# One hybrid decoder layer: VectorE's work on a step's operands is issued behind that of the step before, in the down projection

## The chip, the cores and the metric

One core of a Trainium2 chip runs the whole kernel. TensorE multiplies, with products in PSUM (8 banks of 128x512 float32); VectorE, ScalarE and GpSimd work on elements; the queues of SP and ScalarE issue transfers (DMAs) between HBM and SBUF. Each engine takes its instructions in the order in which the program has them, and waits at one until its inputs are there. The metric is the device time of one execution in microseconds (us); of several runs the median counts.

## What is computed

A layer with three mixers side by side, and a gated MLP behind them:

```python
h = rms_norm(x, norm1_g) * (1 + sc1) + sh1
x = x + g1 * hybrid_mixer(h, ...)            # GLA, retention, stick-breaking
h = rms_norm(x, norm2_g) * (1 + sc2) + sh2
x = x + g2 * swiglu(h, wg, wu, wd)           # (silu(h wg) * (h wu)) wd
return rms_norm(x, final_g)
```

1024 tokens, width 1024, MLP width 2816, all in float32. The change concerns the last product, `(...) wd`, a matrix of 1024x2816 by one of 2816x1024.

## The kernel before

**The down projection.** The product of gate and up projection, called G here, is 1024 tokens by 2816; w_down is 2816 by 1024. Both are cut into halves, G by tokens and by alternate blocks of 128 of the inner dimension, w_down by columns, and the product of the 2x2 blocks is made with seven block products instead of eight (Strassen's scheme in Winograd's form), whose left operands are the blocks a11, a12, a22 and the sums s1 to s4, and whose right operands are blocks of w_down and sums of them. The stage before has written the left ones to HBM (`d_g`).

A *step* (p, j) is one of 4 passes and one of 11 pairs of blocks j; pass 0 makes one of the seven products, passes 1 to 3 two each. `flow` (L1257) lists the steps, (0,0) to (3,10). For each step a generator `prep_1`, `prep_67`, `prep_53` or `prep_24` (L1180 to 1213) prepares operands in two halves: up to its `yield` it issues loads on SP, of `d_g` blocks into tiles `whi` and `wlo` in turn (three of each) and of w_down into a tile `hb` (`b_raw`, four of them; pass 0 loads into `kb[j]`, tiles that in the rows are called `hh` and `hl`). Behind the `yield` VectorE makes two *combining* instructions, as here in pass 2:

```python
tt(DVE, rb[:, 1], rb[:, 0], kb[j], ALU.subtract)      # hb <- hb, hh (or hl)
tt(DVE, kb[j], kb[j], grow[:, :NH], ALU.mult)         # hh <- hh, grow
return [(opnd(ra[:, 0]), opnd(rb[:, 1])), (opnd(ra[:, 1]), opnd(rb[:, 0]))]
```

and then `opnd` (L1147) splits each of the four sources into a rounded part (a cast on ScalarE, L929) and the rest (a *subtract* on VectorE, in `tt`, L58), because a product is made from three matmuls of such parts (`mm3`, L67). The results lie in 18 operand slots used in turn: 12 tiles `to` and 6 pairs made of old `hh` and `hl`. In pass 3 one of the four operands, a12, is ready in HBM and is loaded straight into its slot (`opnd_of`, L1156). A combining instruction needs the load of its `hb`; a cast needs a free slot, that is, the matmuls over 18 operands before.

**Matmuls and adds.** A step makes, for each of its products and each of 4 blocks of 128 tokens, three 128x512 matmuls: 12 in pass 0, 24 in the others. The 4 or 8 PSUM banks of a pass (tiles `m`, `dn`, `tr`) gather all 11 steps. At the end of a pass they are added to `ct` in SBUF (VectorE, `ct<-ct,m` and the like; pass 0 copies them with ScalarE), and a bank is free for the next pass when this is done. Between the steps, residual additions and squares of finished output columns are made (`residual`, `second_columns`: `ct<-ct,grow`, `ct<-ct,raw`, `ct<-ct,st`), with the residual loaded into tiles `raw`. The last three steps of pass 3 are held back and made bank by bank, each followed by its final norm and store (the tail).

**What sets the order.** The program is traced step by step: loads are asked for six steps ahead, operands three steps ahead (four late in pass 3), through `finish` (L1276), which runs a generator's second half. A scheduler then puts each engine's instructions into an order by a simulated timeline of its own: an instruction whose inputs come early there may move ahead of others, also of those of earlier steps.

Of the kernel before, what the change touches and what calls it, by code (L numbers as in the profile page):

```python
# [1 line left out]

# [37 lines left out]
def tile_hybrid(ctx, tc, x, c, ada_w, ada_b, norm1_g, norm2_g, w_in, gla_wa2, gla_ba,  # L40
# [3 lines left out]
    PE, ACT, DVE, POOL = nc.tensor, nc.scalar, nc.vector, nc.gpsimd  # L44
# [10 lines left out]


    def tt(eng, o, a, b, op):
        eng.tensor_tensor(out=o, in0=a, in1=b, op=op)  # L58

    def sub_lo(lo, src, hi):  # L60
        tt(DVE, lo, src, hi.bitcast(F32), ALU.subtract)
# [33 lines left out]
    def rstd_of(dst, ss, n, w):  # L95
        t = const.tile([P, 8], F32, name="rs_t", bufs=2)
        POOL.tensor_scalar(t[:, :w], ss, 1.0 / n, EPS, op0=ALU.mult, op1=ALU.add)
        tt(POOL, dst, t[:, :w], mhalf[:, :w], ALU.pow)
# [20 lines left out]
    def w_load(src, shape, fold=None):  # L119
        nn = shape[1] * shape[2]  # L120
        raw = wp.tile([P, W_SLOT], F32, name="raw", bufs=2)[:, :nn].rearrange("p (a b) -> p a b", a=shape[1])
        if isinstance(src, list):
            n = shape[1] // len(src)
            for i, sr in enumerate(src):
                nc.sync.dma_start(raw[:, i * n:(i + 1) * n], sr)
        else:
            nc.sync.dma_start(raw, src)
        if fold is not None:
            tt(DVE, raw, raw, fold, ALU.mult)
        hi = wp.tile([P, W_SLOT], F32R, name="whi")[:, :nn].rearrange("p (a b) -> p a b", a=shape[1])  # L130
        lo = wp.tile([P, W_SLOT], F32R, name="wlo")[:, :nn].rearrange("p (a b) -> p a b", a=shape[1])
        split(hi, lo, raw)
        return hi, lo
# [785 lines left out]
    def halves(x):  # L919
        return x.rearrange("p (n c) -> p n c", n=2)  # L920
# [147 lines left out]
    for j in range(4):  # L1068
# [5 lines left out]
        for lst, r in ((t2, r22), (t3, r12), (t4, r21)):  # L1074
            op = halves(tp.tile([P, D], F32R, name="to"))
# [197 lines left out]

    loaded = {}

    def finish(gen):  # L1276
        try:
            next(gen)
        except StopIteration as e:
            return e.value  # L1280

    for n, (p_, j) in enumerate(flow):

        for q, jq in flow[n:n + 3 + (p_ == 3 and j > 4)]:
            if (q, jq) not in ready:
                if (q, jq) not in loaded:
                    loaded[q, jq] = passes[q](jq)
                    next(loaded[q, jq])
                ready[q, jq] = finish(loaded[q, jq])
# [94 lines left out]
```

## Time and profile before

| | us |
|---|---|
| median of 3 runs | 1334.87 (1334.02 to 1335.86) |
| the profiled execution | 1338.11 |
| its span, first to last instruction | 1336.3 |
| TensorE busy in the span | 1277.9 (96%) |
| VectorE, ScalarE, GpSimd busy | 883.8, 634.1, 521.9 |
| granted TensorE clock, mean | 0.984 of full |

The down projection takes the end of the span, from about 1109.5 us: pass 0 to 1139.5, pass 1 to 1199.8, pass 2 from 1205.0 to 1266.5, then pass 3 with its tail from 1312. In the views PE is TensorE, DVE VectorE, ACT ScalarE, POOL GpSimd, and SPq the queue of SP. A row of a timeline gives start and duration, and in brackets how long the engine had stood idle before it and what it waited for. A matmul row's duration covers its way through the array, so that what counts is the distance from start to start. Tile names stand without their numbers.

### The profile page before, as it was taken

The numbers are of one execution on the slowest core, as the hardware profiler recorded it, in microseconds if no ns is written. First come the engines' busy times: TensorE is split into PE (matmuls) and PEld (weight loads), VectorE is DVE, ScalarE is ACT, GpSimd is POOL, SyncE is SP. The second block draws the span as 40 slices with busy tenths as digits, with TensorE's granted clock in tenths as the row PEclk, the third lists the DMA queues.
The fourth block names the chain that finished last, engine by engine and source line by source line (L and its number), as shares of the span: only waits on it lengthen the run. The fifth ranks groups of instructions, "written<-read, shape, count | busy, mean of one in ns | idle before, by whom it ended". The sixth has DMA issues, their size and how long they took to land. (4 is left out here: it accounts for less than half of the span.)

```text
span 1336.3 us, 20162 instructions
## 1 busy us (share of the span) xinstructions
PE 1277.9 (96%) x7165; PEld 1095.7 (82%) x7165; DVE 883.8 (66%) x1381; ACT 634.1 (47%) x1254; POOL 521.9 (39%) x594
## 2 busy tenths in 40 slices
PE   6999989998999989988999999999999999999997
PEld 3779988898899988987978888888887888877776
DVE  2424566778867768896678665665565659959695
ACT  3647557766647635453564332332333325443343
POOL 1017425346524354672114555556545432000044
PEclk8999998999999999998999999999999999999999
DMA  9647445444423275122324334343343358834453
GB/s 325 208 140 219 137 111 175 126 109 142 132 81 95 70 232 174 54 82 95 106 103 135 110 111 134 103 137 131 103 133 110 106 190 300 282 118 155 150 186 148
DMA packets 144334, 192.33 MB, mean 144 GB/s; under 512 B 19837, under 2 KB 94918, under 8 KB 144234
## 3 DMA queue, kind: packets, MB, share of 16 engines
q1 hardware_dynamic: 113808, 150.65, 36.7%
q10 hardware_dynamic: 30426, 40.40, 8.5%
q8 instruction: 56, 0.92, 0.3%
q14 instruction: 44, 0.36, 0.1%
HBM read 141.13 MB, written 49.87 MB: 143 GB/s over the span
## 5 line engine op out<-in xcount | busy, mean ns | idle before, releaser
L68 PE MATMUL dn<-whi,hh 128*128 128x256 f32 (+1 forms) x768 | 225.2, 293 | 4.3 <-DVE s_u L431 2.3
L69 PE MATMUL dn<-wlo,hh 128*128 128x256 f32 (+1 forms) x768 | 224.6, 293 | 0.0
L70 PE MATMUL dn<-whi,hl 128*128 128x256 f32 (+1 forms) x768 | 222.3, 290 | 0.0
L68 PEld LDWEIGHTS dn<-whi,hh 128*128 128x128 f32 x768 | 149.7, 195 | 6.3 <-DVE hh L58 2.8
L69 PEld LDWEIGHTS dn<-wlo,hh 128*128 128x128 f32 x768 | 149.8, 195 | 1.6 <-issue 0.2
L70 PEld LDWEIGHTS dn<-whi,hl 128*128 128x128 f32 x768 | 149.4, 195 | 1.2 <-issue 0.2
L58 POOL TENSOR_TENSOR s_a<-s_a,s_u 128x128 f32<-128x128 f32 (+3 forms) x96 | 95.6, 998 | 95.1 <-DVE s_u L434 89.9
L434 DVE TENSOR_TENSOR_SCAN s_u<-z,s_u,zero 128x128 f32<-128x128 f32 (+3 forms) x96 | 96.3, 1008 | 35.8 <-ACT z L427 24.8
L58 POOL TENSOR_TENSOR st<-raw 128x512 f32<-128x512 f32 x40 | 57.9, 1449 | 112.3 <-DMA raw<-in_ffn_wg_dram 86.5
L58 POOL TENSOR_TENSOR x<-x,x 128x512 f32<-128x512 f32 x51 | 70.7, 1388 | 44.8 <-DVE x L58 37.5
L1238 POOL TENSOR_SCALAR ss<-ss 128x1 f32<-128x1 f32 x8 | 22.5, 2814 | 167.5 <-ACT raw L1234 166.9
L64 ACT CAST s_th<-tr 128x512 fp32r<-128x512 f32 (+2 forms) x112 | 48.6, 434 | 54.7 <-PE tr L451 29.3
L58 DVE TENSOR_TENSOR s_tl<-tr,s_th 128x512 fp32r<-128x512 f32 (+2 forms) x112 | 54.6, 487 | 28.1 <-ACT s_th L64 27.8
L929 ACT CAST wlo<-raw 128x512 fp32r<-128x512 f32 x34 | 20.9, 616 | 109.0 <-POOL x L58 82.3
L58 POOL TENSOR_TENSOR grow<-grow,a_raw 128x1024 f32<-128x1024 f32 x24 | 58.4, 2433 | 35.3 <-ACT a_raw L305 21.8
L58 DVE TENSOR_TENSOR wlo<-raw,wlo 128x512 fp32r<-128x512 f32 x34 | 24.5, 720 | 68.1 <-ACT wlo L929 68.1
L58 DVE TENSOR_TENSOR wlo<-st,wlo 128x512 fp32r<-128x512 f32 x40 | 41.2, 1032 | 37.1 <-ACT wlo L929 37.0
L426 ACT ACTIVATE s_a<-z 128x128 f32<-128x128 f32 (+3 forms) x96 | 47.1, 491 | 24.1 <-PE z L424 15.7
L68 PE MATMUL dn<-hh,whi 128*128 128x512 f32 x140 | 56.0, 400 | 1.4 <-ACT st L293 1.4
L70 PE MATMUL dn<-hh,wlo 128*128 128x512 f32 x144 | 56.4, 392 | 0.0
L69 PE MATMUL dn<-hl,whi 128*128 128x512 f32 x140 | 55.3, 395 | 0.0
L58 DVE TENSOR_TENSOR x<-x,m 128x512 f32<-128x512 f32 x68 | 45.6, 679 | 13.8 <-PE m L70 13.8
(395 smaller groups left out, 3830.9 us busy)
## 6 DMA issues: line engine op xcount, KB each, us to landing
a_raw<-in_ada_w_dram SPq DMA_DIRECT2D x24, 512.0 KB, 4.1
raw<-in_ffn_wg_dram SPq DMA_DIRECT2D x22, 512.0 KB, 3.8
raw<-in_ffn_wu_dram SPq DMA_DIRECT2D x22, 512.0 KB, 4.1
d_g_s<-x ACTq DMA_DIRECT2D x44, 256.0 KB, 2.2
hb<-in_ffn_wd_dram SPq DMA_DIRECT2D x44, 256.0 KB, 4.0
raw<-in_w_in_dram SPq DMA_DIRECT2D x20, 512.0 KB, 4.3
aw<-in_ada_w_dram SPq DMA_DIRECT2D x32, 256.0 KB, 6.0
d_g_a<-x ACTq DMA_DIRECT2D x22, 256.0 KB, 3.4
```

Source lines behind the costliest of these rows:

```text
L58: eng.tensor_tensor(out=o, in0=a, in1=b, op=op)
L64: ACT.copy(hi, src)
L68: PE.matmul(o, sh, mh, start=start, stop=False)
L69: PE.matmul(o, sh, ml, start=False, stop=False)
L70: PE.matmul(o, sl, mh, start=False, stop=stop)
L426: ACT.activation(At[:, c0:c0 + w], z[:, :w], AF.Sigmoid, scale=0.125)
L434: DVE.tensor_tensor_scan(ur, z[:, 0:w][:, ::-1], zero.broadcast_to([P, w]), u[:, w:w + 1], op0=ALU.mult, op1=ALU.add)
L929: ACT.copy(op[0], src)
L1238: POOL.tensor_scalar(ss2[t][:, 1:2], ss2[t][:, 1:2], 1.0 / D, EPS, op0=ALU.mult, op1=ALU.add)
```

## The change

`tt` now keeps the last instruction that it made on VectorE. When a step's preparation is over, `finish` notes that instruction, the last subtract of the step; everything that the next step's second half traces on VectorE is put behind the instruction noted last, by an order edge within the engine (`issue_after`). Such an edge carries no wait: it fixes which stands first in VectorE's queue. Loads, casts and the adds of PSUM banks have no such edge; the scheduler orders them anew around it.

```diff
     def tt(eng, o, a, b, op):
-        eng.tensor_tensor(out=o, in0=a, in1=b, op=op)
+        made_tt[eng is DVE] = eng.tensor_tensor(out=o, in0=a, in1=b, op=op)
+
+    made_tt = {}
...
     loaded = {}
 
+    done = []
+
     def finish(gen):
-        try:
-            next(gen)
-        except StopIteration as e:
-            return e.value
+        with (tc.issue_after(done[-1].ins) if done else nullcontext()):
+            try:
+                next(gen)
+            except StopIteration as e:
+                done.append(made_tt[True])
+                return e.value
```

Three places of VectorE's order follow. In the names, the `kb` tiles of pairs j = 0 to 5 are `hh_0_11562`, `hl_0_11572`, `hh_0_11582`, `hl_0_11592`, `hh_0_11596` and `hl_0_11600`, that of j = 10 is `hh_0_11718`.

VectorE at the turn from pass 1 to pass 2, before, from the last subtracts of step (2,1) on:

```order
L58 TENSOR_TENSOR to<-whi,to 128x512
L58 TENSOR_TENSOR to<-hb,to 128x512
L58 TENSOR_TENSOR to<-wlo,to 128x512
L58 TENSOR_TENSOR to<-hb,to 128x512
L58 TENSOR_TENSOR hb<-hb,hl_0_11600 128x512
L58 TENSOR_TENSOR hl_0_11600<-hl_0_11600,grow 128x512
L58 TENSOR_TENSOR to<-wlo,to 128x512
L58 TENSOR_TENSOR to<-hb,to 128x512
L58 TENSOR_TENSOR ct<-ct,m 128x512
```

The same place now, from the same two subtracts on:

```order
L58 TENSOR_TENSOR to<-whi,to 128x512
L58 TENSOR_TENSOR to<-hb,to 128x512
L58 TENSOR_TENSOR hb<-hb,hh_0_11582 128x512
L58 TENSOR_TENSOR hh_0_11582<-hh_0_11582,grow 128x512
L58 TENSOR_TENSOR to<-wlo,to 128x512
L58 TENSOR_TENSOR to<-hb,to 128x512
L58 TENSOR_TENSOR to<-wlo,to 128x512
L58 TENSOR_TENSOR to<-hb,to 128x512
L58 TENSOR_TENSOR hb<-hb,hl_0_11592 128x512
L58 TENSOR_TENSOR hl_0_11592<-hl_0_11592,grow 128x512
L58 TENSOR_TENSOR ct<-ct,m 128x512
```

The combining instructions of (2,5), and of (2,4) and (2,3) before them, no longer stand ahead of the first add; those of (2,2) and (2,3) come directly ahead of their own step's subtracts.

VectorE at the turn from pass 2 to pass 3, before: the combining instructions of (3,4), then of (3,5), with subtracts of (3,1) and (3,2) between and behind them.

```order
L58 TENSOR_TENSOR hb<-hb,grow 128x512
L58 TENSOR_TENSOR hb<-hb,hh_0_11596 128x512
L58 TENSOR_TENSOR to<-wlo,to 128x512
L58 TENSOR_TENSOR to<-hb,to 128x512 x2
L58 TENSOR_TENSOR hb<-hb,grow 128x512
L58 TENSOR_TENSOR hb<-hb,hl_0_11600 128x512
L58 TENSOR_TENSOR hl_1_12930<-whi,hh_1_12929 128x512
L58 TENSOR_TENSOR hl_1_12934<-hb,hh_1_12933 128x512
L58 TENSOR_TENSOR ct<-ct,m 128x512 x2
```

The same place now: step (3,2) whole, the two combining instructions of (3,3), and the adds.

```order
L58 TENSOR_TENSOR hb<-hb,grow 128x512
L58 TENSOR_TENSOR hb<-hb,hh_0_11582 128x512
L58 TENSOR_TENSOR to<-hb,to 128x512
L58 TENSOR_TENSOR hl_1_12930<-whi,hh_1_12929 128x512
L58 TENSOR_TENSOR hl_1_12934<-hb,hh_1_12933 128x512
L58 TENSOR_TENSOR hb<-hb,grow 128x512
L58 TENSOR_TENSOR hb<-hb,hl_0_11592 128x512
L58 TENSOR_TENSOR ct<-ct,m 128x512 x2
```

The combining instructions of (3,4) and (3,5) have moved behind the adds.

VectorE at the end of pass 3, before: the last rows ahead of the tail's first add.

```order
L58 TENSOR_TENSOR hb<-hb,hh_0_11718 128x512
L58 TENSOR_TENSOR to<-hb,to 128x512
L58 TENSOR_TENSOR ct<-ct,raw 128x512
L58 TENSOR_TENSOR ct<-ct,st 128x512
L58 TENSOR_TENSOR to<-wlo,to 128x512
L58 TENSOR_TENSOR to<-hb,to 128x512
L58 TENSOR_TENSOR ct<-ct,raw 128x512
L58 TENSOR_TENSOR to<-hb,to 128x512
L58 TENSOR_TENSOR ct<-ct,st 128x512 x2
L58 TENSOR_TENSOR ct<-ct,raw 128x512
L58 TENSOR_TENSOR to<-whi,to 128x512
L58 TENSOR_TENSOR to<-hb,to 128x512
```

The same place now: the whole of steps (3,9) and (3,10).

```order
L58 TENSOR_TENSOR hb<-hb,grow 128x512
L58 TENSOR_TENSOR hb<-hb,hl_0_11694 128x512
L58 TENSOR_TENSOR to<-hb,to 128x512
L58 TENSOR_TENSOR to<-wlo,to 128x512
L58 TENSOR_TENSOR to<-hb,to 128x512
L58 TENSOR_TENSOR hb<-hb,grow 128x512
L58 TENSOR_TENSOR hb<-hb,hh_0_11718 128x512
L58 TENSOR_TENSOR to<-hb,to 128x512
L58 TENSOR_TENSOR to<-whi,to 128x512
L58 TENSOR_TENSOR to<-hb,to 128x512
```

The residual work stands ahead of these steps now, and the combining instructions of (3,10) directly ahead of its three subtracts.

## Rows read from the trace of the kernel before

**Rows 1.** The page's first part: busy time, share, instructions of each engine.

```profile
PE 1277.9 (96%) x7165; PEld 1095.7 (82%) x7165; DVE 883.8 (66%) x1381; ACT 634.1 (47%) x1254; POOL 521.9 (39%) x594
```

**Rows 2.** By stretch: busy (count) of PE, PEld, DVE, ACT, POOL; clock; DMA; GB/s.

```profile
1139.50:1199.80 60.30, 60.17 (x265) 49.27 (x263) 46.48 (x76) 28.47 (x51) 0.00 (x0) 1.00 0.59 195
1266.50:1312.20 45.70, 44.35 (x193) 35.92 (x193) 41.28 (x69) 17.40 (x37) 22.51 (x8) 1.00 0.53 171
```

**Rows 3.** Waits of TensorE from 1099 us on: total, times, longest.

```profile
PE m L68 <- DVE ct L58: 5.0, 1, 5.0
PE m L68 <- DMA hh<-d_g_a12h: 1.1, 1, 1.1
```

**Rows 4.** Timeline of TensorE at the turn from pass 1 to 2: start, duration.

```profile
1194.85 0.39 PE L70 MATMUL m<-to 128*128 128x512 f32 x1
...
1199.61 0.39 PE L70 MATMUL m<-to 128*128 128x512 f32 x1
1205.01 0.77 PE L68 MATMUL m<-hh,hh 128*128 128x512 f32 x1 [5.01 <-DVE ct L58]
...
1208.32 0.39 PE L70 MATMUL m<-to 128*128 128x512 f32 x1
```

**Rows 5.** By stretch, as rows 2, just behind that wait.

```profile
1205.00:1208.40 3.40, 3.39 (x9) 2.72 (x10) 2.87 (x6) 0.00 (x0) 0.00 (x0) 0.56 0.61 210
```

**Rows 6.** Timeline of VectorE up to the turn from pass 1 to 2.

```profile
1175.39 0.69 DVE L58 TENSOR_TENSOR hb<-hb,hl 128x512 f32<-128x512 f32 x1 [2.03 <-DMA hb<-in_ffn_wd_dram]
...
1194.60 0.69 DVE L58 TENSOR_TENSOR hb<-hb,hh 128x512 f32<-128x512 f32 x1 [2.34 <-DMA hb<-in_ffn_wd_dram]
...
1196.54 0.68 DVE L58 TENSOR_TENSOR to<-hb,to 128x512 fp32r<-128x512 f32 x1
...
1201.64 0.69 DVE L58 TENSOR_TENSOR hb<-hb,hl 128x512 f32<-128x512 f32 x1 [3.21 <-DMA hb<-in_ffn_wd_dram]
...
1204.18 0.68 DVE L58 TENSOR_TENSOR ct<-ct,m 128x512 f32<-128x512 f32 x1
```

**Rows 7.** Timeline of SP's queue there: issue of the load for (2,5).

```profile
1197.54 0.38 SPq L1140 DMA_DIRECT2D hb<-in_ffn_wd_dram  x1
```

**Rows 8.** The tile `hb` from 1100 us on: waits for its loads, and landing times.

```profile
  DMA hb<-in_ffn_wd_dram: 29.9, 17
...
DMA to landing us min/median/max: 2.9/4.0/6.5
```

**Rows 9.** Timeline of ScalarE there: first cast of each half of (2,3).

```profile
1194.64 0.62 ACT L929 CAST to<-whi 128x512 fp32r<-128x512 f32 x1 [1.58 <-issue]
...
1197.36 0.62 ACT L929 CAST to<-whi 128x512 fp32r<-128x512 f32 x1 [1.58 <-issue]
```

**Rows 10.** Timeline of TensorE at the turn from pass 2 to 3.

```profile
1266.32 0.39 PE L70 MATMUL m<-to 128*128 128x512 f32 x1
...
1270.15 0.47 PE L68 MATMUL m<-hh,hh 128*128 128x512 f32 x1 [1.07 <-DMA hh<-d_g_a12h]
...
1271.39 0.39 PE L68 MATMUL m<-to 128*128 128x512 f32 x1
```

**Rows 11.** Timeline of VectorE there: the wait for (3,5), the last subtract of (3,2).

```profile
1262.88 0.69 DVE L58 TENSOR_TENSOR hb<-hb,grow 128x512 f32<-128x512 f32 x1 [2.26 <-DMA hb<-in_ffn_wd_dram]
...
1264.82 0.68 DVE L58 TENSOR_TENSOR hl<-hb,hh 128x512 fp32r<-128x512 f32 x1
```

**Rows 12.** Timeline of SP's queue there.

```profile
1265.53 0.33 SPq L1140 DMA_DIRECT2D hb<-in_ffn_wd_dram  x1
...
1266.43 0.38 SPq L1165 DMA_DIRECT2D hl<-d_g_a12l  x1
```

**Rows 13.** Timeline of TensorE at the turn from pass 0 to 1.

```profile
1142.64 0.39 PE L70 MATMUL m<-to 128*128 128x512 f32 x1
1143.16 0.50 PE L68 MATMUL tr<-to 128*128 128x512 f32 x1
```

**Rows 14.** By stretch, as rows 2: pass 3 until VectorE's operands are done.

```profile
1269.00:1309.50 40.50, 39.24 (x172) 32.07 (x172) 40.09 (x67) 16.78 (x36) 22.12 (x6) 1.00 0.55 176
```

More of the change, by code (lines that the diff above doesn't have):

```diff
@@ L1 @@
-from contextlib import ExitStack
+from contextlib import ExitStack, nullcontext
 import concourse.bass as bass
```

## The prediction

> **What bounds the kernel now.** The page's first part says that TensorE is the bound: busy for 1277.9 of 1336.3 us, VectorE for 883.8 [rows 1]. The change touches only the down projection, so the table by stretch comes next. There TensorE starts one matmul after another: 265 in the 60.3 us of pass 1, 0.2275 us from start to start; VectorE is busy for 46.5 of these 60.3 us, and for 41.3 of the 45.7 us of pass 3 before its last three steps [rows 2]. So only a hole in TensorE's row is worth anything in this stage. From 1099 us to the end TensorE has one long wait, 5.0 us for VectorE's `ct`, and short ones for loads of `a12`, the longest 1.1 us [rows 3].
>
> The long one stands at the turn from pass 1 to pass 2. The last matmul of pass 1 starts at 1199.61, the next one at 1205.01 [rows 4]; from then to 1208.4 the granted clock is 0.56, about 1.2 instead of 2.4 GHz, after the engine had stood still [rows 5]. What is waited for is a PSUM bank: `ct<-ct,m` adds the product of pass 1 into SBUF and frees the bank. Its matmuls were over at 1195.24 (the third starts at 1194.85 and takes 0.39) [rows 4], but the add ran at 1204.18 [rows 6], 8.9 us late. VectorE's own row says why: before it in the queue stand the two combining instructions of step (2,5), `hb<-hb,hl` and `hl<-hl,grow`, and the first sat 3.21 us until its load of w_down landed [rows 6]. That load was issued at 1197.54 [rows 7], right after VectorE's last subtract of step (2,1) (1196.54, 0.68 us) [rows 6], which gave its `hb` buffer back: there are four, so step j+4 loads into that of step j. The instruction is queued where its load cannot be there yet. Five such waits in a row, 2.0 to 3.2 us each and some 13 us together, lead up to the turn [rows 6]; in the whole down projection they are 17, 29.9 us [rows 8].
>
> **The change part by part.** No instruction is added or removed on any engine. VectorE's work on the operands of a step now stands behind the last subtract of the step before it, as the order listings show; loads keep their places on SP but for residual tiles and a few `hb`.
>
> (a) *From pass 1 to pass 2.* Ahead of the first `ct<-ct,m` the last combining instructions are now those of (2,3), no longer of (2,5). The casts that the subtracts follow go by TensorE's release of operand slots: the pairs at 1194.64 and 1197.36 are the two halves of (2,3), 2.72 us apart, which is 12 matmuls [rows 9]; the last pair of (2,2) is one beat earlier, at about 1191.9. With 0.60 us from one VectorE instruction to the next (67 in 40.1 us [rows 14]), (2,2) is through at about 1194, and (2,3)'s two combining instructions at about 1195.2. The load for (2,3) takes the buffer of (1,10), three steps of 5.46 us before; loads land after 4.0 us in the median [rows 8], so it is there. The add runs at about 1195.3, as its matmuls end, and the bank is free 4 us before TensorE asks. What is won: from the start at 1199.61 to that at 1208.32 lie nine starts and 8.71 us [rows 4]; at 0.2275 they take 2.05. **6.66 us**, 1.6 of it the slow clock.
>
> (b) *From pass 2 to pass 3.* From 1266.32 to 1271.39 TensorE has 13 starts in 5.07 us, at 0.2275 2.96: 2.11 us are lost, most where step (3,3) wants its `a12` at 1270.15 [rows 10]. That load stands on SP behind the `hb` load for step (3,6), which waits for VectorE's last subtract of (3,2): 1264.82 [rows 11], then `hb` at 1265.53 and the second half of `a12` at 1266.43 [rows 12]. VectorE was late because it had sat 2.26 us for the load of (3,5) [rows 11]. Nothing of (3,3) to (3,5) stands ahead of these subtracts now. Their casts are due three half steps before the pass ends, 8.2 us, so that the subtracts are through some 6.3 us before the end, not 1.7; `a12` comes 4.6 us earlier against the turn, and was short by 1.1. **2.11 us**; its bounds are 0 and 2.11, and I take the upper one, since the margin of 3.5 us is wide.
>
> (c) *From pass 0 to pass 1.* ScalarE copies two `tr` banks here, and now has one cast between the two copies. TensorE lost 0.29 us (0.52 from start to start) [rows 13]. The first bank comes free sooner, the second a cast (0.62 us [rows 9]) later: between -0.4 and +1 us, taken as 0, as the two work against each other.
>
> (d) *Where the order costs.* VectorE can no longer spend a wait for a cast on a later step's combining. In pass 1 it has room [rows 2], and operands are ready some four steps ahead (18 slots, four a step). Pass 3 is tight: in the listing of before, 70 instructions stand from the first add at the turn to the last ahead of the tail, and VectorE runs without rest from 1269 to 1309.5 [rows 14], where TensorE begins the last three steps at about 1312.3. Now 74 stand there, 44.4 us at 0.60; but they begin about 4.7 us before the turn, not 1.1. They end 39.7 us after it, and TensorE wants the last one 45 us after it: 5 us of cover. Cost: nothing.
>
> **Sum.** 6.66 + 2.11 = 8.77 us. The profiled execution took 1338.11 us, 1.81 beyond its span; it would take 1329.3. The runs' median is 1334.87, 3.24 lower. Of that, what is not the 1.81 may be shorter holes without the profiler; I take half of those 1.43 off the gain: 8.05 us, **1326.8**.
>
> **The rivals.**
> *Both turns mended*: 1326.8, between 1325.7 (the full gain, and the -0.4 of (c)) and 1329.3 (all of the 3.24 off the gain). Chance 0.60.
>
> *Only the first.* `a12` still lands after it is wanted, since SP keeps it behind the `hb` load, whose loads take up to 6.5 us [rows 8]. Against it: VectorE's late subtract held it, and that moves. 2.11 less: 1328.9. Chance 0.10.
>
> *The first in part.* A wait for a cast takes the place of that for a load: two subtracts of (2,3) stand between the first and the second add. If they came only with the second pair of casts (1197.36), the adds of all eight banks would end some 3 us after the turn, and half of the hole would stay: 1330 to 1332. Chance 0.08.
>
> *The holes are the profiler's.* VectorE's waits build up because a step takes it 7.04 us (1194.60 to 1201.64) [rows 6] where TensorE takes 5.46. The shortest load of `hb` took 2.9 us [rows 8]; if all did without the profiler, each of the five waits were 1.1 us shorter, the add 3.4 us late and not 8.9, which the 4.6 us between its matmuls' end and the end of the pass would swallow. Then the runs have no long hole to lose, and 2.1 us are won at most: 1332.8 to 1335.5. For it: loads spread from 2.9 to 6.5 us. Against it: the median of 4.0, and only 3.24 us lie between profile and runs. Chance 0.15. The Trainium skill (DMA: Bandwidth & Descriptors, Latency and other measured facts) says that a DMA's fixed cost shrinks as the load on HBM falls, with 0.2 us for an access on average and 2 us at high load. By that rule a run without the profiler's writes would lose up to 1.8 us of each load, an estimate from that page, and so the whole hole; no run here shows a load without the profiler.
>
> *Slower.* VectorE becomes the bound in pass 3. Before, it kept the waits for loads off the end by working ahead. If each of the six steps (3,5) to (3,10) still sat 2.3 to 3.2 us for its loads, 14 to 19 us would come to its 44.4, 9 to 14 beyond the cover, and TensorE would stand as long before its last steps and restart slowly (1.6): less 8.05, 1337.5 to 1342.5, say 1339.5. It decides from 5 us of such waits on. Against it: a load is issued when VectorE is done four steps earlier, 16 us ahead of its use in step order. Chance 0.07.
>
> That the order isn't what the change says is ruled out by the listings.
>
> **How the numbers follow.** A measurement of this kernel can tell about 0.2% (2.7 us) from nothing. Faster by more: 0.60 + 0.10 + 0.08 and a fifth of the profiler's case, 0.81. Same 0.12, slower 0.07. The range starts at 1324.5, 1325.7 less some 1 us, by which single runs lie under their median, and reaches over the third case to 1333.0; it leaves out the slower case and most of the profiler's.
>
> **What would show it.** Right: TensorE has no wait for `ct` after 1099 us; no stretch between the passes under clock 1; the first `ct<-ct,m` runs within 1 us of the end of its matmuls; VectorE's waits for `hb` loads fall from 29.9 us to a few, and waits for ScalarE's casts take their place; `a12` of (3,3) lands before it is wanted. Wrong: a wait of TensorE for an operand (`to`, `hl`) in pass 3, or VectorE's last subtract within 1 us of TensorE's last three steps; or a span shorter by 9 us while the runs are not.

## The result

The changed kernel takes 1328.17 us in the median of five runs (1323.22 to 1329.29), the kernel before, run beside it, 1335.12 (1334.02 to 1338.21). That is 6.95 us less by the medians. The ratio of the two kernels' runs is 0.994, with a 95% interval of 0.9921 to 0.9958: some 8 us less (5.6 to 10.5), where 8.05 had been forecast, and 1.4 us more than the 1326.8 named. The profiled execution is the first of the five runs and also took 1328.17 us. Its first part answers to [rows 1]:

```profile
PE 1273.4 (96%) x7165; PEld 1093.2 (82%) x7165; DVE 885.6 (67%) x1381; ACT 634.2 (48%) x1254; POOL 509.2 (38%) x594
```

The instruction counts are those of [rows 1]. From 1099 us on, TensorE's waits answer to [rows 3]:

```profile
PE tr L70 <- ACT ct L1315: 0.9, 2, 0.6
```

The 5.0 us for `ct` and the 1.1 us for `a12` are gone; what is left stands at the turn from pass 0 to pass 1. TensorE at the turn from pass 1 to pass 2, where [rows 4] had 5.40 us between two starts:

```profile
1198.07 0.39 PE L72 MATMUL m<-to 128*128 128x512 f32 x1
1198.30 0.39 PE L70 MATMUL m<-hh,hh 128*128 128x512 f32 x1
```

Now it is 0.23 us, and the matmuls behind it run at the same distance: there is no slow clock (granted clock 1.00 from 1198.2 to 1208). VectorE there, as [rows 6] (start, duration, wait in brackets):

```profile
1191.04 0.69 DVE L58 TENSOR_TENSOR to<-wlo,to 128x512 fp32r<-128x512 f32 x1 [1.43 <-ACT to L931]
1191.65 0.68 DVE L58 TENSOR_TENSOR to<-hb,to 128x512 fp32r<-128x512 f32 x1
1192.25 0.68 DVE L58 TENSOR_TENSOR hb<-hb,hl 128x512 f32<-128x512 f32 x1
1192.96 0.69 DVE L58 TENSOR_TENSOR hl<-hl,grow 128x512 f32<-128x512 f32 x1
1193.74 0.69 DVE L58 TENSOR_TENSOR ct<-ct,m 128x512 f32<-128x512 f32 x1
```

The combining instructions of (2,3) start without a wait, and the first add follows them 4.6 us before TensorE asks for the bank (1198.30); in [rows 6] it came 4.6 us after the last matmul of the pass. Over the down projection VectorE now waits for casts, where [rows 8] had 29.9 us for loads of `hb`; its waits from 1099 us on begin so, and no `hb` load is among them:

```profile
DVE to L58 <- ACT to L931: 16.8, 12, 3.7
DVE ct L58 <- PE m L72: 5.2, 3, 4.8
DVE hl L58 <- ACT hh L931: 4.7, 3, 1.8
```

At the turn from pass 2 to pass 3, SP's queue and TensorE, as [rows 12] and [rows 10]:

```profile
1253.30 0.38 SPq L1167 DMA_DIRECT2D hl<-d_g_a12l  x1
```

```profile
1260.19 0.39 PE L72 MATMUL m<-to 128*128 128x512 f32 x1
1260.42 0.39 PE L70 MATMUL m<-hh,hh 128*128 128x512 f32 x1
```

The second half of `a12` is issued 7.1 us before (3,3) begins, and TensorE goes on at 0.23 us.

**Where the 9.9 us between the two spans lie.** The profiled spans differ by 9.9 us (1336.3 and 1326.4), more than the 8.77 us that both holes cost. The first matmul of the down projection and the last of the kernel, before and after:

```profile
1109.48 0.62 PE L68 MATMUL tr<-to 128*128 128x512 f32 x2
...
1328.57 0.39 PE L70 MATMUL m<-to 128*128 128x512 f32 x1
```

```profile
1106.81 0.62 PE L70 MATMUL tr<-to 128*128 128x512 f32 x2
...
1318.28 0.39 PE L72 MATMUL m<-to 128*128 128x512 f32 x1
```

From the one to the other are 219.09 us before and 211.47 after: 7.6 us were won in the stage that was changed, 2.7 us stood ahead of it, where the stage began earlier in this execution, and the end behind the last matmul took 0.4 us more. This stretch, the *stage time* below, is what the experiments are compared by. It holds 924 matmuls (7 products, 11 steps, 4 token blocks, 3 parts), and 923 distances of 0.2275 us are 210.0 us.

### The profile page after: what moved, and what is told of

Read it like the earlier page. It is cut to its first block, busy times and chain, and to the rows that moved or that the text cites. A ratio compares the mean times of both kernels' runs of the same rounds, so it can differ in the third digit from the quotient of the medians.

```text
span 1326.4 us, 20148 instructions
## 1 busy us (share of the span) xinstructions
PE 1273.4 (96%) x7165; PEld 1093.2 (82%) x7165; DVE 885.6 (67%) x1381; ACT 634.2 (48%) x1254; POOL 509.2 (38%) x594
## 4 chain that ended last, share of the span: by engine, by line
PE 63%; DVE 5%; DMA 4%; ACT 3%; issue 2%; POOL 1%; SPq 0%; ACTq 0%; POOLq 0%; DVEq 0%
PE dn L70 7%; PE dn L71 7%; PE dn L72 7%; PE m L70 7%; PE m L72 7%; PE m L71 7%; PE tr L70 4%; PE tr L71 4%; PE tr L72 4%; PE tr L453 1%; DVE hl L58 1%; PE g L629 1%; DVE to L58 1%; DMA hl<-in_ffn_wd_dram 1%; PE av L473 1%
## 5 line engine op out<-in xcount | busy, mean ns | idle before, releaser
L436 DVE TENSOR_TENSOR_SCAN s_u<-z,s_u,zero 128x128 f32<-128x128 f32 (+3 forms) x96 | 96.3, 1009 | 34.5 <-ACT z L429 22.2
L1240 POOL TENSOR_SCALAR ss<-ss 128x1 f32<-128x1 f32 x8 | 11.9, 1493 | 164.6 <-ACT raw L1236 164.4
L58 DVE TENSOR_TENSOR wlo<-raw,whi 128x1024 fp32r<-128x1024 f32 (+2 forms) x34 | 45.2, 1334 | 16.1 <-ACT whi L66 16.1
```

The costliest lines, as they stand in the source:

```text
L58: made_tt[eng is DVE] = eng.tensor_tensor(out=o, in0=a, in1=b, op=op)
L436: DVE.tensor_tensor_scan(ur, z[:, 0:w][:, ::-1], zero.broadcast_to([P, w]), u[:, w:w + 1], op0=ALU.mult, op1=ALU.add)
L1240: POOL.tensor_scalar(ss2[t][:, 1:2], ss2[t][:, 1:2], 1.0 / D, EPS, op0=ALU.mult, op1=ALU.add)
```

## The experiments

All kernels with the stage time of their trace, beside the medians. "Turn 0-1" is what TensorE loses there beyond its rhythm of start to start; "hb" the waits of VectorE for loads of `hb` from 1099 us on. Ratios are against the kernel before on the same chip: for the change itself the runs of the section above, then a median of 1334.40 (23 runs) from all_edges_again to one_edge_2_5, 1334.25 (16) from edges_pass2_only to before_again, 1332.45 (11) for the last two. The diffs below show the decisive line against the changed kernel, and for no_load_needed against the kernel before; handing `q` and `jq` to `finish` is left out.

| kernel | median us | ratio (95%) | stage begins | stage time | turn 0-1 | hb |
|---|---|---|---|---|---|---|
| before (first trace) | | | 1109.48 | 219.09 | 0.4 | 29.9 |
| the change (first trace) | 1328.17 | 0.994 (0.9921 to 0.9958) | 1106.81 | 211.47 | 1.5 | 0 |
| all_edges_again | 1324.09 | 0.9935 (0.9919 to 0.9950) | 1106.61 | 210.27 | 0.3 | 0 |
| edges_from_pass2 | 1324.89 | 0.9933 (0.9919 to 0.9948) | 1103.71 | 211.28 | 0.8 | 2.3 |
| edges_pass3_only | 1334.57 | 0.9997 (0.9982 to 1.0011) | 1106.89 | 219.45 | 1.0 | 16.6 |
| one_edge_2_5 | 1330.32 | 0.9979 (0.9966 to 0.9992) | 1105.84 | 214.35 | 1.2 | 25.5 |
| edges_pass2_only | 1325.73 | 0.993 (0.9913 to 0.9946) | 1103.88 | 210.94 | 1.0 | 3.5 |
| two_edges | 1328.17 | 0.9953 (0.9935 to 0.997) | 1104.63 | 212.04 | 1.0 | 24.3 |
| no_load_needed | 1325.07 | 0.9928 (0.9911 to 0.9945) | 1105.28 | 211.45 | 0.8 | 14.3 |
| before_again | 1335.10 (one run) | | 1104.25 | 221.32 | 1.1 | 31.0 |
| lag_2 | 1326.24 | 0.9955 (0.9937 to 0.9972) | 1104.03 | 211.83 | 1.9 | 0 |
| lag_3 | 1326.54 | 0.9949 (0.9933 to 0.9964) | 1104.44 | 209.96 | under 0.1 | 2.9 |

**The two kernels once more.** No edit to either.

> The kernel before once more, for a second trace, since its first one (1338.11) stands at the long end of its runs, 1329.8 to 1339.4. Theory: both holes are in every execution, 5.2 us and its slow clock at the turn from pass 1 to 2 and 2.1 us at the turn from pass 2 to 3, each within 1 us, and the executions differ ahead of the down projection. Rival: the first trace caught long holes, and another execution has the second one, or both, shorter by half.

> The changed kernel once more, to see how its runs spread (the first five lie in two groups, 1323 to 1324 and 1328 to 1329) and whether the profile repeats. Theory: both holes of the down projection are gone in every execution, so that TensorE waits for less than 2 us from 1099 us on, and the spread of some 5 us comes from stretches ahead of the down projection, in which the granted clock differs. Median 1324 to 1329, ratio to the kernel before 0.992 to 0.996. Rival: the spread is in the down projection, with a hole that opens in some executions.

Both holes of the kernel before are there again; its waits of TensorE from 1099 us on:

```profile
PE m L68 <- DVE ct L58: 4.6, 1, 4.6
PE m L68 <- ACT to L929: 1.4, 1, 1.4
PE tr L68 <- ACT ct L1307: 0.8, 1, 0.8
PE tr L69 <- DVE to L58: 0.8, 1, 0.8
PE m L68 <- DMA hh<-d_g_a12h: 0.7, 1, 0.7
```

The one at the turn from pass 1 to 2 costs 6.1 us with its slow clock (6.66 in the first trace), the ones about the turn from pass 2 to 3 cost 2.8 us (1.9 to 2.1); a late VectorE shows here also as a late cast. The changed kernel lost nothing at either of these turns in both of its traces. Against the mean of both traces of before, 220.2, the stage is 9.3 us shorter in the mean of both traces after, 210.9.

The second trace of before begins the stage 5.2 us earlier than the first, and yet spends 2.2 us more in it. The 1338.11 us of the first execution thus say nothing on the size of its holes: what made it long lies ahead of the stage, which begins anywhere from 1103.7 to 1109.5 us in the twelve traces. What differs there was not tried. Nor do the two traces of the changed kernel settle the spread of its runs: both come from longer executions (1328.17 and 1326.74 us), none from those of 1323 to 1324, and of the 1.4 us between the two, 1.2 lie in the stage, at the turn from pass 0 to 1. In the five runs of the changed kernel in the section above, the two short ones have a mean granted clock of 0.989 and 0.990, the three long ones 0.987 and 0.988, but the kernels of the table do not rank by it (0.991 with one_edge_2_5).

**Passes apart.**

```diff
-        with (tc.issue_after(done[-1].ins) if done else nullcontext()):
+        with (tc.issue_after(done[-1].ins) if done and q > 1 else nullcontext()):
```

with `q > 1` in the first kernel, `q == 3` in the second, `q == 2` in the third.

> The order edge only for the steps of passes 2 and 3; the steps of passes 0 and 1 are as in the kernel before. VectorE's order at the turns from pass 1 to 2 and from 2 to 3 is that of the changed kernel, and ScalarE's two copies of tr at the turn from pass 0 to 1 stand together again. Theory: both holes are gone, and at the turn from pass 0 to 1 TensorE loses 0.3 to 0.4 us, as in the kernel before, and not 1.5: the span is 1.1 us shorter than with all edges, which the medians can hardly show (ratio 0.992 to 0.995). Rival: the 1.5 us have another cause than the cast between the copies; then they stay. Waits of VectorE for hb loads come back in pass 1 only.

> The order edge only for the steps of pass 3. Up to the turn from pass 1 to 2 VectorE's order is that of the kernel before. Theory: the two holes are separate, each with its own cause. The one of 5.0 us at the turn from pass 1 to 2 stays, with its slow clock behind; the 2.1 us at the turn from 2 to 3 are won, as a12 of (3,3) lands in time: 2.1 us less than before, 1333.0. Rival: the second hole is a late echo of the first (SP's queue was late ever since); then it stays too and the time is that of before, 1335.1. Second rival: pass 3 in step order costs something that the changed kernel hid; then the time is above 1335.

> The order edge only for the steps of pass 2; in pass 3 VectorE works ahead again, as in the kernel before. Theory: the hole of 5 us at the turn from pass 1 to 2 and its slow clock are gone, the lateness of a12 of (3,3) is back with 1 to 2 us: 6.7 us less than before, 1327.7, and 2 us more than with all edges. Rival: nearly all of the gain of the whole change is in pass 2, since the edges of pass 3 alone brought the median nothing (1334.57 against 1334.4): 1325 to 1326. In the trace the rival shows no wait for a12.

Edges from pass 2 on are as good as all. But at the turn from pass 0 to 1 this kernel lost 0.8 us, though ScalarE copies its two `tr` banks one behind the other again, and the changed kernel, with its cast between them, lost 1.5 us in one trace and 0.3 in the other. The cast between the copies is not what sets this loss: it goes from nothing to 1.9 us over the ten traces in which the copies stand together. That part of the theory fell; what sets the loss is told under (c) below.

Pass 3 alone brought the median nothing that can be measured; the expected 2.1 us lie just inside the interval (0.9982 is 2.4 us). Its trace has the first hole, and no wait about the turn from pass 2 to 3:

```profile
PE m L70 <- DVE ct L58: 4.7, 1, 4.7
PE tr L71 <- DVE to L58: 0.8, 1, 0.8
PE tr L70 <- ACT ct L1315: 0.7, 1, 0.7
```

So the second hole was mended in the trace. The stage time doesn't show it against the first trace of before, because this execution lost 2.1 us in pass 0 and at its turn (0.4 there) and its slow clock behind the first hole lasted longer; against the second trace of before, which lost 2.2 us in the same early places, it is 1.9 us shorter.

Pass 2 alone brings all: the rival of that run was right. Its waits of TensorE from 1099 us on, and VectorE's for `hb`:

```profile
PE tr L70 <- ACT ct L1315: 0.7, 1, 0.7
```

```profile
DVE hb L58 <- DMA hb<-in_ffn_wd_dram: 3.5, 6, 1.2
```

In pass 3 VectorE works ahead again here, and the combining instructions of (3,4) and (3,5) again stand ahead of the adds; yet none of them waits for more than 0.8 us, and `a12` of (3,3) is in time. One more thing moved here: on SP, `a12` of (3,3) now stands ahead of the `hb` load that it follows in [rows 12]:

```profile
1249.82 0.38 SPq L1167 DMA_DIRECT2D hl<-d_g_a12l  x1
1250.30 0.38 SPq L1142 DMA_DIRECT2D hb<-in_ffn_wd_dram  x1
```

It is issued 7.1 us before it is wanted (1256.93). In the old order it would have come 0.90 us behind that `hb` load [rows 12], 5.7 us ahead by this estimate, and some 3.6 would have done (2.5 us in the kernel before, which was short by 1.1). So the place on SP is not what mends the hole: VectorE comes to these steps earlier. Either set of edges mends the second hole; only that of pass 2 mends the first.

**One edge, and two.**

```diff
-        with (tc.issue_after(done[-1].ins) if done else nullcontext()):
+        with (tc.issue_after(done[-1].ins) if done and (q, jq) == (2, 5) else nullcontext()):
```

and `(q, jq) in ((2, 5), (3, 5))` for two.

> One order edge in the whole program: VectorE's work of step (2,5) behind the last subtract of (2,4). Around the turn from pass 1 to 2 this moves two instructions, the combining ones of (2,5), from ahead of the first add of a PSUM bank to behind it; VectorE's other hoisted instructions stay. Theory: only the one wait that stands ahead of the adds costs time. The first add runs at about 1198.4 instead of 1204.2, before the pass ends; 6.0 to 6.7 us are won (1328.5 to 1329.1), though VectorE's waits for hb loads in the down projection fall only by some 3 of 29.9 us. The 2.1 us at the turn from 2 to 3 stay lost. Rival: the gain goes with the sum of these waits; then a tenth of it is won, under 1 us, and the time is above 1334. Second rival: the two adds that stand behind casts come late and half of the hole stays: 1331 to 1332.

> Two order edges: (2,5) behind (2,4), and (3,5) behind (3,4). To the kernel with one edge this adds that the two combining instructions of (3,5) stand behind the adds at the turn from pass 2 to 3. Theory: VectorE's last subtract of (3,2) no longer sits behind the load of (3,5), so a12 of (3,3) is issued some 2.3 us earlier and lands before it is wanted; 1.2 to 2 us less than with one edge (1330.3): 1328.3 to 1329.1. Rival: VectorE's other waits for loads, some 20 us that stay, hold it late all the same, and TensorE waits for a cast or for a12 near this turn as with one edge (two waits of 0.9 us): 1330.3 again.

With one edge VectorE goes from the wait for the load of (2,4), through three pairs of subtracts, to the add:

```profile
1191.35 0.69 DVE L58 TENSOR_TENSOR hb<-hb,hh 128x512 f32<-128x512 f32 x1 [2.25 <-DMA hb<-in_ffn_wd_dram]
...
1196.30 0.68 DVE L58 TENSOR_TENSOR ct<-ct,m 128x512 f32<-128x512 f32 x1
```

TensorE starts the last matmul of pass 1 at 1196.81 and the first of pass 2 at 1197.13: over this turn it loses 0.7 us in all, with 25.5 us of VectorE's waits still present. That is the theory's mechanism; a gain in step with the sum of the waits (under 1 us) is out. Its size was missed: of the 6.0 to 6.7 us expected, the median shows 4.1 us and the ratio 2.8 (1.1 to 4.5). In the traces the stage is 4.7 us shorter than in the first of before and 7.0 shorter than in the second. What is missing against the first is 0.7 us left of the hole, 0.8 more at the turn from pass 0 to 1, and 0.4 more at the turn from pass 2 to 3:

```profile
PE m L70 <- ACT to L931: 0.9, 1, 0.9
PE m L70 <- DMA hh<-d_g_a12h: 0.9, 1, 0.9
PE tr L70 <- ACT ct L1315: 0.9, 1, 0.9
PE dn L70 <- DVE ct L58: 0.2, 1, 0.2
```

VectorE is still late through pass 2, and TensorE waits 0.9 us for a cast at 1258, which the first trace of before had not. The second edge ends this wait and that for `a12`: the stage is 2.3 us shorter than with one edge, and the second half of `a12` of (3,3) is issued 148.6 us after the stage's begin instead of 152.7.

```profile
PE tr L70 <- ACT ct L1315: 0.7, 1, 0.7
PE dn L70 <- DVE ct L58: 0.3, 1, 0.3
```

Two edges stay 2 us behind the change by the ratios, with intervals that overlap. Why runs of these two kernels spread further than those of the changed one (1328.6 to 1335.5, and 1323.4 to 1333.7) was not settled; each has one trace.

**The wait taken away, the order left.**

```diff
-        tt(DVE, rb[:, 1], rb[:, 0], kb[j], ALU.subtract)
+        tt(DVE, rb[:, 1], kb[j], kb[j], ALU.add)
         tt(DVE, kb[j], kb[j], grow[:, :NH], ALU.mult)
```

> The kernel before, without order edges; in pass 2 the first combining instruction of a step adds the tile kb to itself and no longer reads the w_down block that was loaded for the step, so that this part of the product is not what the layer asks for. The load is still made, with the same bytes, and is read later by a cast. Instructions and transfers are as many as before; VectorE now stands even further ahead: the combining instructions of (2,6) too are ahead of the first add. Theory: the place ahead of the adds costs nothing in itself, only a wait for a load there does. VectorE has no wait for an hb load up to the turn from pass 1 to 2, the first add runs within 2 us of its matmuls' end, the hole of 5 us is gone: 6 to 6.7 us less than before, 1327.7 to 1328.4. Rival: the hoisted work itself, eight instructions of 0.6 us of steps (2,3) to (2,6), makes the add late; then a hole of 2 us or more stays and the time is 1331 or more.

The theory held: 9.6 us less by the ratio, more than the 6 to 6.7 expected, since the second hole went too. VectorE's first add stands behind the combining instructions of (2,6), a step further ahead than in the kernel before:

```profile
1190.82 0.69 DVE L58 TENSOR_TENSOR hb<-hh 128x512 f32<-128x512 f32 x1
1191.55 0.69 DVE L58 TENSOR_TENSOR hh<-hh,grow 128x512 f32<-128x512 f32 x1
1192.19 0.69 DVE L58 TENSOR_TENSOR ct<-ct,m 128x512 f32<-128x512 f32 x1
```

and this add ends 3.9 us before pass 2 begins (1196.75). Work ahead of the adds cost nothing by itself; the waits for loads in it did. This run takes away all such waits of pass 2, not only the last. The 14.3 us of waits for `hb` that are left belong to steps of pass 1 (two) and of pass 3 (seven, up to 2.9 us each, from 1221 us on). Even so the second half of `a12` of (3,3) was issued 4.8 us before it was wanted (1254.02, 1258.82), in the kernel before 2.5 and in the changed one 7.1: VectorE was on time when these waits began, and what they made it late by stayed within the margin. SP's order is that of [rows 12] here.

**How far ahead is too far.**

```diff
-        with (tc.issue_after(done[-1].ins) if done else nullcontext()):
+        with (tc.issue_after(done[-2].ins) if len(done) >= 2 else nullcontext()):
```

and 3 for 2 in the other.

> A looser order: VectorE's work of a step is put behind the last subtract of the step two before it, so that it may work one step ahead. An hb buffer is given back by step n and loaded for step n+4; here at least two whole steps of subtracts, some 10.9 us of TensorE's pace, lie between the two in VectorE's queue, and loads land after 4.0 us in the median, 6.5 at the most. Theory (what costs is the distance between the release of a buffer and the use of its next load): VectorE waits less than 3 us in all for hb loads, no hole, the down projection takes 211 us, 1325.3. Rival (any work ahead costs): waits of 8 to 12 us, a quarter to a third of those of before, and 2 to 3 us more than with the change: 1328.

> The order looser again: behind the last subtract of the step three before. The combining instructions of (2,5) stand ahead of the first add of a PSUM bank once more, as in the kernel before, directly so; but two subtracts of (2,2), which in the kernel before stood behind them, stand ahead of them. Between a buffer's release and the use of its next load lies at least half a step, 2.7 us, up to a whole one. Theory: the wait for a load shrinks from 2 to 3 us to what 4.0 us of landing leave over, 1.3 us or less at one place; VectorE waits 3 to 12 us in all for hb loads, never more than 2 us at once, the first add is in time and the holes are gone or under 1 us: 1325 to 1327. Rival: it is enough that this instruction stands ahead of the adds; then the hole of some 5 us is back, waits are 20 us and more, and the time is 1331 to 1334.

Both theories held in the main. With a lag of 2 VectorE has no wait for `hb` and neither of the two holes is there; of the stage's 211.83 us, 1.9 are lost at the turn from pass 0 to 1. With a lag of 3 the combining instructions of (2,5) stand directly ahead of the first add, as near to it as in [rows 6]:

```profile
1182.30 0.68 DVE L58 TENSOR_TENSOR to<-hb,to 128x512 fp32r<-128x512 f32 x1
...
1187.13 0.69 DVE L58 TENSOR_TENSOR to<-wlo,to 128x512 fp32r<-128x512 f32 x1 [1.43 <-ACT to L931]
1187.74 0.69 DVE L58 TENSOR_TENSOR to<-hb,to 128x512 fp32r<-128x512 f32 x1
1188.34 0.68 DVE L58 TENSOR_TENSOR hb<-hb,hl 128x512 f32<-128x512 f32 x1
1189.06 0.69 DVE L58 TENSOR_TENSOR hl<-hl,grow 128x512 f32<-128x512 f32 x1
1189.83 0.69 DVE L58 TENSOR_TENSOR ct<-ct,m 128x512 f32<-128x512 f32 x1
```

The `hb` of (2,5) is released by the last subtract of (2,1), as before. In [rows 6] and the listing of before, one pair of subtracts of (2,2) stood between that and the use of its next load; now the combining instructions of (2,4) and both pairs stand there, and these follow casts and so TensorE's pace. The release is over at 1182.98, 5.4 us ahead of the use; in [rows 6] VectorE had come to that use 1.2 us after the release (1197.22, and 1201.64 less the wait of 3.21). The load has landed, there is no wait, and the add comes 4.6 us before pass 2 begins (1194.39). The earlier waits of pass 2 are gone with it, so that this run shows the distance at work in all steps together, not in (2,5) alone. All of VectorE's waits for `hb` are three:

```profile
DVE hb L58 <- DMA hb<-in_ffn_wd_dram: 2.9, 3, 2.3
```

Their sum is slightly under the 3 to 12 us expected, and one, at a step of pass 1, is longer than the 2 us named. The stage takes 209.96 us, what its matmuls need at their rhythm, so that no hole is left in it. Its ratio is no better than the others for that (6.8 us less): none of the versions beats the change by more than their intervals.

## Why the prediction was right

**The signs.** All that were named for being right came, but for one in its words: TensorE still has a wait for `ct`, 0.9 us for ScalarE's copies at the turn from pass 0 to 1. None of those for being wrong came: the spans of the traces are 9.9 us shorter, and the runs are shorter too.

**(a) From pass 1 to pass 2: right.** Hole and slow clock are gone. The order of events came as worked out: the pass ends 1.54 us earlier in this trace than in the first (1198.07 against 1199.61), so the add, predicted for about 1195.3 there, was due at 1193.8, and ran at 1193.74. The cause is shown from three sides: the instruction moved alone (one_edge_2_5), the wait taken away with the order left (no_load_needed), more paced work between release and use (lag_3) each close the hole. Up to the first add, VectorE's order in the first of these differs from that of before by two instructions alone. In [rows 6] the add runs only after the instruction that waited 3.21 us, though its matmuls had ended 8.9 us before. The Trainium skill (PSUM — Partial Sum Buffer, Engine vs sequencer instructions) states that the queues of ScalarE, VectorE and GpSimd are strictly first in, first out. Those rows agree with it. Only a size was slightly off: the slow clock behind the hole cost 1.5 us from start to start in that trace, not 1.6.

**(b) From pass 2 to pass 3: right in size, its cause only in part.** `a12` is issued 7.12 us before it is wanted (1253.30, 1260.42), and in the kernel before 2.50 us (1266.43, and 1268.93, where the matmul behind that of 1268.70 would have started): 4.6 us earlier against the turn, as worked out. But the prediction put this to the combining instructions of (3,3) to (3,5), which no longer stand ahead of the subtracts. Taking that away is enough (edges_pass3_only), but it is not needed: with edges in pass 2 alone, and with the loads of pass 2 not waited for (no_load_needed), those of (3,4) and (3,5) still stand ahead of the adds, with waits of up to 0.7 and 2.4 us, and the hole is mended as well. By these runs the hole took both, a VectorE that came late out of pass 2 and the waits for loads of pass 3 on top. The prediction read the last link of the chain of waits as the whole.

**(c) From pass 0 to pass 1: the value was good by luck, the reason not.** Zero was taken because a copy moved up and another moved back a cast. The first trace after has 1.5 us against 0.4, just beyond the bound of 1 us more; the second has 0.3, the second of before 1.1. The second copy, the one behind its cast, accounts for 0.5 and 0.2 us of the two losses after. The rest goes by when ScalarE comes to its first copy, and that copy stands behind casts that wait, the same pattern as in (a). The traces with the least and the greatest loss, lag_3 (none) and lag_2 (1.9 us), begin the stage at 1104.44 and 1104.03:

```profile
1135.43 0.62 ACT L931 CAST hh<-hl 128x512 fp32r<-128x512 f32 x1 [3.56 <-DVE hl L58]
1137.00 1.06 ACT L1315 COPY ct<-tr 128x512 f32<-128x512 f32 x2
```

```profile
1136.98 0.62 ACT L931 CAST hh<-hl 128x512 fp32r<-128x512 f32 x1 [3.23 <-PE dn L72]
1138.54 1.06 ACT L1315 COPY ct<-tr 128x512 f32<-128x512 f32 x2
```

In all ten traces with both copies together this cast stands three places ahead of the first copy, and waits 3.2 to 5.3 us, for VectorE's combining instruction in nine of them. Measured from the stage's begin, less what TensorE had lost up to there, the copy starts after 32.6 us (lag_3) to 34.5 (lag_2), and the loss grows with that start to within 0.1 us. The bound had looked at the place of the copies among the casts, not at what the casts ahead of them wait for. No kernel here has the copies ahead of these casts, so that a remedy is not shown.

**(d) Where the order costs: right that it costs nothing, with less cover than worked out.** VectorE's last subtract, then TensorE's first matmul of the last three steps and its first of (3,10):

```profile
1299.53 0.68 DVE L58 TENSOR_TENSOR to<-hb,to 128x512 fp32r<-128x512 f32 x1
```

```profile
1302.04 0.39 PE L70 MATMUL m<-hh,hh 128*128 128x512 f32 x1
1303.41 0.39 PE L70 MATMUL m<-to 128*128 128x512 f32 x1
```

Pass 3 begins at 1258.38. VectorE is through 41.8 us later (1300.21), not 39.7, and TensorE wants (3,10) 45.0 us later, as worked out: 3.2 us of cover, not 5. One us of the difference is a wait for a residual's load, which the sum had not. The slower case needed 5 us and more of waits for the loads of (3,5) to (3,10), and there were none.

**The sum.** 8.77 us off the first trace's stage time of 219.09 gives 210.32; the traces after have 211.47 and 210.27, and the first owes its surplus to (c). What does not hold is the last step: the 3.24 us between the profiled execution and the median were taken as a sign that holes might be shorter elsewhere, and 0.7 us came off the gain. Every run's time is 1.8 us over its own span, so that the 1.81 are no part of the 3.24; and a long execution is not one with long holes (before_again). The 0.7 us are too small for the runs to check: the gain is 6.95 us by the first medians and 10.3 by those of the repetition, and 9.3 by the stage. That 8.05 lies this close to the 8 us of the ratio is partly luck.

**The rivals.** Only the first hole mended: out, by the rows of the second turn. The first in part: out, by those of the first. The holes are the profiler's: its time (1332.8 to 1335.5) is out, and the gain of the stage in the traces, 9.3 us, is found again in the times, 8.0 and 8.7 us by the two ratios. But each run here comes with a span and a granted clock, so that no run here shows an execution without the records; what the holes are without them stays open. That rival leaned on a rule of the Trainium skill (DMA: Bandwidth & Descriptors, Latency and other measured facts) on a DMA's fixed cost under load. The loads of `hb` landed after 3.7 to 4.2 us in the median of every trace, and no run here shows a load without the profiler.

## What to carry to other kernels

On an engine that takes its instructions in order, look at what a waiting instruction holds up, not at how long it waits: 24 of some 30 us of waits could stay at a cost of 1 to 2 us (two_edges), while one wait of 3 us ahead of the adds that free PSUM banks cost over 6 in the traces of the kernel before. A load that refills a buffer has the time between the release of that buffer and its use in the same queue; count the instructions between the two, and where they are too few, put work between them that goes at TensorE's pace, rather than forbid working ahead (here 5.4 us from release to use were enough, and 1.2 were not). And compare executions by a stretch that the change can reach, from one fixed matmul to another: the executions compared here differed by 2.7 and by 5.2 us ahead of it, at the most more than half of the effect.

## What the runs showed of the hardware

The slow clock behind a stand-still of TensorE does not last equally long. After waits of 5.0 us (before), 4.6 (before_again) and 4.7 (edges_pass3_only) at the same place, the rhythm was back after 3.1, 2.7 and 5.3 us. In the last, the stretch reads so (busy of PE, PEld, DVE, ACT, POOL; clock; DMA; GB/s):

```profile
1203.80:1209.00 5.20, 5.17 (x12) 4.13 (x13) 4.69 (x8) 0.00 (x0) 0.00 (x0) 0.50 0.40 141
```

The clock is 1.2 instead of 2.4 GHz for all of it, and stand-stills of nearly the same length cost 1.5, 1.3 and 2.5 us behind them. A price read from one execution is thus one of several that occur.
